# One core, two decoder layers: the first norm's row first, low-priority warm-ups, a standing VectorE, softmax sums on VectorE, twelve weight slots

## The chip, the cores and the metric

The kernel runs on one core of a Trainium2 chip. The time is device microseconds of one execution. The core's engines run their own instruction streams in order and wait for each other by semaphores: TensorE (PE; its weight loads are shown as PEld), VectorE (DVE), ScalarE (ACT), GpSimd (POOL) and SyncE (SP), which issues the DMAs.

## The reference

A decoder trunk of two layers on 256 tokens of width 1024, float32. Cut to what is computed:

```python
for layer in range(2):
    h = h + 0.5 * swiglu(rms_norm(h, ffn1_norm[layer]), ffn1_w_in[layer], ffn1_w_out[layer])
    hn = rms_norm(h, mix_norm[layer])
    if layer == 0:      # 16 heads of 64
        q, k, v = split(hn @ sb_w_qkv)
        h = h + stick_breaking_attention(q, k, v) @ sb_w_o
    else:               # 16 query heads, 4 key/value heads, window 128, one sink a head
        q = rotary(hn @ swa_w_q)
        h = h + sliding_window_sink_attention(q, k_shared, v_shared, sinks) @ swa_w_o
    h = h + 0.5 * swiglu(rms_norm(h, ffn2_norm[layer]), ffn2_w_in[layer], ffn2_w_out[layer])
    if layer == 0:
        k_shared, v_shared = rotary(k), v   # of rms_norm(h, kv_norm) @ kv_w
return rms_norm(h, final_norm)

def swiglu(x, w_in, w_out):                 # w_in 1024 x 5632, w_out 2816 x 1024
    gate, up = split(x @ w_in)
    return (silu(gate) * up) @ w_out
```

`rms_norm` is x * rsqrt(mean(x*x) + 1e-6) * gain. The softmax of the window runs over 256 keys at most, masked to the band, and the sink's logit.

## The kernel before

**Split products.** Activations and weights are split in two parts each, a high part rounded to the type fp32r and a low part that is the rest; a product is three matmuls (high x high, low x high, high x low), each 128 rows by 512 columns. A weight comes as a block of 1 MB into one of 4 `raw` slots (`RAWS`, 8 KB a partition). ScalarE copies it to the high part (`w_hi`, L324), VectorE subtracts to get the low part (`w_lo`, L326), both in two pieces of 1024 columns. The parts lie in `2 * PAIRS` = 10 slots (`WP`); a pair is released when TensorE has used it. v, q and k of the first attention, q of the second and the operands of the shared keys and values take slots of the same ten.

**Stages.** Two token tiles (t = 0, 1) of 128. A feed-forward block goes through 2816 columns in six blocks (`BLOCKS`): "p" (plain, 512), "h" (narrow, 256) and "s" (one level of Strassen over two halves of the depth and the token tiles, 512); the "s" blocks need sums of the activations' quarters, made once a layer by `make_sums` (L450 to L456). Its last two blocks' output products run tile by tile, and after each tile comes `fin`: `add_residual` (L422), `root` and `normed`.

**The norm.** `root(t)` has ScalarE square both halves with a sum (L399), VectorE add the two sums (`base`, L401) and GpSimd raise the result to the power -0.5 (`rstd`, L403). `normed` has VectorE scale each half of 512 by `rstd` and the gain (`xs`, L411); TensorE transposes it (L375), ScalarE copies the high part (L381), VectorE makes the low part (L382).

**The order.** Nothing runs in the order in which it is written. Each piece of work is a `Task` with an engine, an assumed duration, the buffers it reads and writes, and a due time `prio`. `Plan.order` plays all tasks through in time: an engine that is free takes the ready task with the smallest `prio`, never waiting for a better one, and a task becomes ready a fixed latency after those it depends on. The instruction streams are then issued in that order, and each engine keeps to it. `plan.pos` is the due time so far, which only dense matmuls advance. Splits are due 7 us ahead of it (`LEAD`), loads 30 us (`LOADS`), the Strassen sums 14 us (`SUMS`).

**The start.** Nine tasks of six warm-up matmuls each go first on TensorE (`warm_up`, due -9e5, into bank 3). SP issues the four quarters of x, the first gain row (4 KB, one partition, `grow`), the first 256 KB piece of each of the first four weight blocks, the next gain, and the other pieces. `spread` brings the row onto all 128 partitions by a matmul with a row of ones, into banks 6 and 7 (`g0`). Later gains are loaded onto all partitions by DMA (512 KB).

**The banded softmax** (`heads` in `sliding_window`): eight times for two heads, TensorE makes the scores and adds the mask, VectorE takes the maxima (L899, L900) and the negated bias (L902), ScalarE four exponentials, each with its sum (L909, `accum_out`), TensorE transposes (L918 to L920), ScalarE and VectorE copy (L386, L925), TensorE multiplies by v. After four times `outputs` adds the sink's exponential to the sums (`SM`), takes the reciprocal and scales (L948 to L955).

Of the kernel before, what the change touches and what calls it, by code (L numbers as in the profile page):

```python
# [35 lines left out]
PAIRS = 5  # L36
RAWS = 4
PIECES = 2

# [4 lines left out]
class Task:  # L44
    __slots__ = ("eng", "dur", "fn", "prio", "deps", "outs", "left", "ready", "start", "end", "seq")

    def __init__(self, eng, dur, fn, prio, seq):
# [22 lines left out]
class Plan:  # L70
# [3 lines left out]
    def add(self, eng, dur, fn, r=(), w=(), prio=None):  # L74
        t = Task(eng, dur, fn, self.pos if prio is None else prio, len(self.tasks))
        for b, k in r:
            if k in b.w:
                t.deps.add(b.w[k])
            else:
                t.deps.update(b.base)  # L80
        for b, k in w:
            if k in b.w:
                t.deps.add(b.w[k])
            else:
                t.deps.update(b.base)
# [12 lines left out]
    def order(self):
# [11 lines left out]
        while True:  # L110
# [21 lines left out]
            for o in t.outs:  # L132
                lat = 0.0 if o.eng == e and e != "SP" else LAT[e]
                o.ready = max(o.ready, t.end + lat)
                o.left -= 1
                if o.left == 0:
                    heapq.heappush(wait[o.eng], (o.ready, o.seq, o))
# [21 lines left out]
def kernel(  # L159
# [74 lines left out]
    one_row = pool.tile([1, P], F32, name="one_row")  # L234
# [6 lines left out]

    def warm_up(n):
        for i in range(n):
            mm(ps_all[:, 3, 0:S], warm.to_broadcast([P, P]), warm.to_broadcast([P, S]), True, True)
# [3 lines left out]
    for i in range(9):  # L248
        T("PE", 900, lambda: warm_up(6), r=[(consts, "warm")], w=B(banks[3]), prio=-9e5 + i)
# [39 lines left out]
    def dma(src, dst, nbytes, w, prio, name=None):  # L289
        T("SP", nbytes / 250.0, lambda: nc.sync.dma_start(out=dst(), in_=src), w=w, prio=prio)  # L290
# [103 lines left out]
    def root(t):  # L394
# [3 lines left out]
        for j in range(2):  # L398
            T("ACT", act(512), lambda j=j: ACT.activation(out=sq.ap, in_=hN.ap[:, t, half(j)], func=AF.Square, scale=1.0 / 32.0,  # L399
                                                          accum_out=ssq.ap[:, j:j + 1]), r=[(hN, (t, j))], w=[(ssq, j), (sq, 0)])  # L400
        T("DVE", 170, lambda: DVE.scalar_tensor_tensor(out=base.ap, in0=ssq.ap[:, 0:1], scalar=EPS, in1=ssq.ap[:, 1:2],  # L401
                                                       op0=ALU.add, op1=ALU.add), r=[(ssq, 0), (ssq, 1)], w=B(base))
        T("POOL", 900, lambda: POOL.tensor_tensor(out=rstd.ap, in0=base.ap, in1=mhalf, op=ALU.pow),  # L403
          r=B(base) + [(consts, "mhalf")], w=B(rstd))
# [3 lines left out]
    def normed(t, rstd, g, pair, dh, dl):  # L408
        for j in range(2):
            xs = STG.get([P, 512], F32, "xs")  # L410
            T("DVE", dve(512), lambda j=j, xs=xs: DVE.scalar_tensor_tensor(  # L411
                out=xs.ap, in0=hN.ap[:, t, half(j)], scalar=rstd.ap, in1=g.ap[:, half(j)], op0=ALU.mult, op1=ALU.mult),
                r=[(hN, (t, j))] + B(rstd, g), w=B(xs))
# [14 lines left out]
    def ffn(w_in, w_out, acc, rest, finish, kv=None, blocks=BLOCKS, first=False):  # L428
# [422 lines left out]
    def sliding_window(w_q, w_o, p0, others_, finish):  # L851
# [31 lines left out]
        def heads(g, i):  # L883
# [22 lines left out]
            for t in (1, 0):  # L906
                for par in range(2):
                    sl_ = slice(par * 384 + (1 - t) * S, par * 384 + 384 - t * P)
                    T("ACT", act(P + t * P, True) + 190, lambda t=t, par=par, sl_=sl_: ACT.activation(  # L909
                        out=e.ap[:, sl_], in_=z[par].ap[:, (1 - t) * S:384 - t * P], func=AF.Exp,  # L910
                        bias=view(NM, t, t + 1, hd + par, hd + par + 1).rearrange("p t h -> p (t h)"),
                        accum_out=view(SM, t, t + 1, hd + par, hd + par + 1).rearrange("p t h -> p (t h)")),
                        r=B(z[par]) + [nk, (consts, "tbl")], w=[(e, (par, t)), (SM, (n, par, t))])
# [26 lines left out]
        def outputs(j):  # L940
# [3 lines left out]
            SS = [(SM, (n, par, t)) for n in range(4 * j, 4 * j + 4) for par in range(2) for t in range(NT)]  # L944
# [32 lines left out]
    def load_x(t, j):  # L977
        dma(xs_[:, t, half(j)], lambda: hN.ap[:, t, half(j)], P * 512 * 4, [(hN, (t, j))], -9e5)
# [35 lines left out]
    T("POOL", 10, lambda: None, r=B(g0), w=B(banks[6], banks[7]))  # L1014
# [71 lines left out]
```

## Time and profile before

| | |
|---|---|
| median of 3 runs | 960.07 us (958.43 to 960.18) |
| profiled execution | 958.79 us, its span 957.0 us |
| mean granted TensorE clock | 0.994 |
| busy: PE, DVE, ACT, POOL | 940.1, 769.1, 566.5, 17.0 us |
| HBM read | 170.67 MB, 179 GB/s over the span |

The span runs from the first to the last instruction of the program. The busy time of an engine is the union of its instructions; matmuls are pipelined and their ends modelled, so a busy TensorE may still be slowed. "A <- B" in a list of waits says that an instruction of A was waiting until one of B had ended; the numbers behind it are the total in us, the times, and the longest. In the chain of waits, each piece is what the next one waited for, back from the end. A line number is that of the kernel before; where a helper issues many operations they share its line (L217 is every matmul).

### The profile page before, as it was taken

Reading aid. Unit: us, or ns where it says so; the run is one execution under the profiler, and the core shown is the slowest. Engines: PE = TensorE matmul, PEld = TensorE weight load, DVE = VectorE, ACT = ScalarE, POOL = GpSimd, SP = SyncE. Lnnn points to the kernel's source line nnn. Section 1 sums busy time; section 2 is a strip of 40 time slices with the busy share of each in tenths; the row PEclk is TensorE's granted clock in tenths of the full one; section 3 lists DMA queues with packets and bytes.
Section 4 is the critical chain, followed back from the end, with each engine's and each line's share of the span. In section 5 each row is a group of like instructions: output and inputs, shape, how many; then the busy total and the mean of one; then the engine's idle time right before and its main releaser. Section 6 shows DMA issues by size and latency. Waiting matters only on the chain.

```text
span 957.0 us, 11930 instructions
## 1 busy us (share of the span) xinstructions
PE 940.1 (98%) x4658; PEld 777.8 (81%) x4658; DVE 769.1 (80%) x876; ACT 566.5 (59%) x783; POOL 17.0 (2%) x30
## 2 busy tenths in 40 slices
PE   9999999999999999999999999999998999999996
PEld 6888888889897888888887888888877888888885
DVE  6888799775556998699978797899875689869993
ACT  6556467556667656556655566557745465655662
POOL 1000000000000000000000000000100000000000
PEclk8999999999999999999999999999999999999998
DMA  8929272853434537634856348256652333762441
GB/s 287 323 92 308 101 264 105 291 200 130 136 130 132 198 132 269 214 101 164 299 192 216 129 168 284 91 206 213 230 194 89 109 112 133 256 228 91 173 176 44
DMA packets 81258, 172.48 MB, mean 180 GB/s; under 512 B 3249, under 2 KB 19889, under 8 KB 81202
## 3 DMA queue, kind: packets, MB, share of 16 engines
q1 hardware_dynamic: 81202, 171.73, 52.6%
q8 instruction: 36, 0.59, 0.3%
q14 instruction: 20, 0.16, 0.0%
HBM read 170.67 MB, written 1.05 MB: 179 GB/s over the span
## 4 chain that ended last, share of the span: by engine, by line
PE 93%; DVE 4%; ACT 1%; issue 1%; POOL 0%; POOLq 0%; DVEq 0%; ACTq 0%
PE ps L217 89%; DVE w_lo L326 2%; PE ps L489 2%; PE ps L375 1%; ACT w_hi L324 0%; DVE xs L411 0%; DVE hN L422 0%; DVE xT_l L382 0%; POOL small L403 0%; DVE raw L580 0%; ACT ws L386 0%; PE ps L919 0%; PE ps L918 0%; PE ps L920 0%; DVE s L456 0%
## 5 line engine op out<-in xcount | busy, mean ns | idle before, releaser
L326 DVE TENSOR_TENSOR w_lo<-raw,w_hi 128x1024 fp32r<-128x1024 f32 x388 | 456.2, 1218 | 70.1 <-ACT w_hi L324 67.2
L324 ACT CAST w_hi<-raw 128x1024 fp32r<-128x1024 f32 x388 | 388.8, 1050 | 106.7 <-PE ps L217 52.9
L217 PE MATMUL ps<-w_hi,xT_h 128*128 128x512 f32 x528 | 210.0, 398 | 0.8 <-ACT w_hi L324 0.8
L217 PE MATMUL ps<-w_hi,xT_l 128*128 128x512 f32 x528 | 206.7, 391 | 0.9 <-DVE xT_l L382 0.9
L217 PE MATMUL ps<-w_lo,xT_h 128*128 128x512 f32 x528 | 206.7, 392 | 0.4 <-DVE w_lo L326 0.4
L217 PE MATMUL ps<-w_hi,aT_h 128*128 128x512 f32 x352 | 140.5, 399 | 0.0
L217 PE MATMUL ps<-w_lo,aT_h 128*128 128x512 f32 x352 | 137.7, 391 | 0.4 <-DVE w_lo L326 0.4
L217 PE MATMUL ps<-w_hi,aT_l 128*128 128x512 f32 x352 | 137.1, 390 | 0.0
L217 PEld LDWEIGHTS ps<-w_lo,xT_h 128*128 128x128 f32 x528 | 99.5, 188 | 22.5 <-DVE w_lo L326 1.6
L217 PEld LDWEIGHTS ps<-w_hi,xT_l 128*128 128x128 f32 x528 | 99.7, 189 | 21.5 <-DVE xT_l L382 2.0
L217 PEld LDWEIGHTS ps<-w_hi,xT_h 128*128 128x128 f32 x528 | 99.6, 189 | 21.4 <-ACT w_hi L324 1.2
L580 DVE TENSOR_TENSOR raw<-raw 128x1024 f32<-128x1024 f32 x96 | 113.8, 1216 | 0.0
L217 PEld LDWEIGHTS ps<-w_lo,aT_h 128*128 128x128 f32 x352 | 66.1, 188 | 15.1 <-DVE w_lo L326 0.9
L217 PEld LDWEIGHTS ps<-w_hi,aT_l 128*128 128x128 f32 x352 | 66.2, 188 | 12.8
L217 PEld LDWEIGHTS ps<-w_hi,aT_h 128*128 128x128 f32 x352 | 66.2, 188 | 12.5
L217 PE MATMUL ps<-w_hi,S_h 128*128 128x512 f32 x192 | 74.7, 389 | 0.0
L217 PE MATMUL ps<-w_hi,S_l 128*128 128x512 f32 x192 | 74.7, 389 | 0.0
L217 PE MATMUL ps<-w_lo,S_h 128*128 128x512 f32 x192 | 74.7, 389 | 0.0
L381 ACT CAST aT_h<-ps 128x512 fp32r<-128x512 f32 (+1 forms) x48 | 26.5, 551 | 78.5 <-PE ps L489 78.5
L477 ACT ACTIVATE m<-ps 128x512 f32<-128x512 f32 (+1 forms) x36 | 19.9, 552 | 39.0 <-PE ps L217 38.7
L217 PEld LDWEIGHTS ps<-w_lo,S_h 128*128 128x128 f32 x192 | 36.0, 188 | 7.5
L217 PEld LDWEIGHTS ps<-w_hi,S_h 128*128 128x128 f32 x192 | 36.0, 188 | 7.5
(158 smaller groups left out, 992.7 us busy)
## 6 DMA issues: line engine op xcount, KB each, us to landing
raw<-in_ffn_w_in_dram SPq DMA_DIRECT2D x76, 1024.0 KB, 5.2
raw<-in_ffn_w_out_dram SPq DMA_DIRECT2D x44, 1024.0 KB, 5.1
raw<-in_sb_w_qkv_dram SPq DMA_DIRECT2D x12, 1024.0 KB, 5.5
raw<-in_ffn_w_in_dram SPq DMA_DIRECT2D x16, 512.0 KB, 4.6
raw<-in_ffn_w_in_dram SPq DMA_DIRECT2D x16, 256.0 KB, 5.4
raw<-in_sb_w_o_dram SPq DMA_DIRECT2D x4, 1024.0 KB, 4.9
raw<-in_swa_w_q_dram SPq DMA_DIRECT2D x4, 1024.0 KB, 7.6
raw<-in_swa_w_o_dram SPq DMA_DIRECT2D x4, 1024.0 KB, 5.3
```

Of the source, the lines that this page charges most:

```text
L217: PE.matmul(ps, lhsT=lhsT, rhs=rhs, start=start, stop=stop, skip_group_check=True)
L324: T("ACT", act(m), lambda sl=sl: ACT.copy(out=flat(hi)[:, sl], in_=flat(raw)[:, sl]), r=[(raw, i) for i in ks], w=[(hi, i) for i in ks], p ...
L326: T("DVE", dve(m), lambda sl=sl: DVE.tensor_sub(out=flat(lo)[:, sl], in0=flat(raw)[:, sl], in1=flat(hi)[:, sl].bitcast(F32)), r=[(raw, i) ...
L375: PE.transpose(out=bank.ap[:, i * P:(i + 1) * P], in_=s, identity=ident)
L381: T("ACT", act(n), lambda: ACT.copy(out=hi[2](), in_=src()), r=B(bank), w=[hi[0:2]])
L477: T("ACT", act(n), lambda: ACT.activation(out=dst(), in_=src(), func=AF.Silu), r=r + [(consts, "tbl")], w=w)
L489: PE.transpose(out=tr.ap[:, i * P:(i + 1) * P], in_=m.ap[:, i * P:(i + 1) * P], identity=ident)
L580: T("DVE", dve(m), lambda sl=sl: DVE.tensor_sub(out=flat(dst)[:, sl], in0=flat(x_)[:, sl], in1=flat(y_)[:, sl]), r=[(b, k) for b in (x_, y ...
```

## The change

- **First row first.** `grow` is loaded from ScalarE's queue as that queue's first task, with a planned latency of its own (`lat`); SP's early DMAs are planned at 330 bytes per ns, and the pieces of the first weight blocks are in order of need, with x's second tile after two pieces of the first block. Gains are due 20 us after the position at which they are asked for, not 30 us before.
- **Warm-ups.** 18 tasks, 8 of two and 10 of four matmuls (56 in all, before 54), due last of all (9e5) and into bank 5; the planner places them where TensorE has nothing else ready. The 18 precede the first other use of bank 5.
- **The first feed-forward's sums** are due 5 us ahead (`FSUMS`).
- **VectorE stands still.** In `fin` the sum, the power and the scaling of the first half are one task of VectorE; its stream holds nothing between the sum and the scaling that waits for GpSimd. The norms at the very start and the final one stay as they were.
- **Banded softmax.** The exponentials have no `accum_out`; two VectorE reductions a time (512 and 256 columns), due 2 us later than their place, make the sums.
- **Twelve slots** (`PAIRS` 6). The scratch that is kept for software-made DMAs is set to 1024 bytes.
- `one_row` becomes a column of ones, broadcast; the task that frees banks 6 and 7 now also counts as a write of `g0`.

```diff
-PAIRS = 5
+PAIRS = 6
+FSUMS = 5000.0
+WARM = 18
...
-                lat = 0.0 if o.eng == e and e != "SP" else LAT[e]
+                lat = t.lat if t.lat is not None else 0.0 if o.eng == e and e != "SP" else LAT[e]
...
-            mm(ps_all[:, 3, 0:S], warm.to_broadcast([P, P]), warm.to_broadcast([P, S]), True, True)
+            mm(ps_all[:, 5, 0:S], warm.to_broadcast([P, P]), warm.to_broadcast([P, S]), True, True)
...
-    for i in range(9):
-        T("PE", 900, lambda: warm_up(6), r=[(consts, "warm")], w=B(banks[3]), prio=-9e5 + i)
+    for i in range(WARM):
+        T("PE", 430, lambda n=2 if i < 8 else 4: warm_up(n), r=[(consts, "warm")], w=B(banks[5]), prio=9e5 + i)
...
-        T("SP", nbytes / 250.0, lambda: nc.sync.dma_start(out=dst(), in_=src), w=w, prio=prio)
+        T("SP", nbytes / (330.0 if prio < -8e5 else 250.0), lambda: nc.sync.dma_start(out=dst(), in_=src), w=w, prio=prio)
...
-        dma(vec.unsqueeze(0).to_broadcast([P, D]), lambda: g.ap, P * D * 4, B(g), plan.pos - LOADS)
+        dma(vec.unsqueeze(0).to_broadcast([P, D]), lambda: g.ap, P * D * 4, B(g), plan.pos + 20000)
...
-                        [(raw, c * 2 // a)], plan.pos - LOADS if c else -8.5e5)
+                        [(raw, c * 2 // a)], plan.pos + 10 * c - 8.5e5)
...
-    def root(t):
+    def root(t, then=None):
...
-        T("DVE", 170, lambda: DVE.scalar_tensor_tensor(out=base.ap, in0=ssq.ap[:, 0:1], scalar=EPS, in1=ssq.ap[:, 1:2],
-                                                       op0=ALU.add, op1=ALU.add), r=[(ssq, 0), (ssq, 1)], w=B(base))
-        T("POOL", 900, lambda: POOL.tensor_tensor(out=rstd.ap, in0=base.ap, in1=mhalf, op=ALU.pow),
-          r=B(base) + [(consts, "mhalf")], w=B(rstd))
+        def mean():
+            DVE.scalar_tensor_tensor(out=base.ap, in0=ssq.ap[:, 0:1], scalar=EPS, in1=ssq.ap[:, 1:2], op0=ALU.add, op1=ALU.add)
+
+        def power():
+            POOL.tensor_tensor(out=rstd.ap, in0=base.ap, in1=mhalf, op=ALU.pow)
+
+        R = [(ssq, 0), (ssq, 1), (consts, "mhalf")]
+        if then:
+            dur, fn, r, w = then
+
+            def run():
+                mean()
+                power()
+                fn(rstd)
+            T("DVE", 1100 + dur, run, r=R + r, w=B(base, rstd) + w)
+        else:
+            T("DVE", 170, mean, r=R, w=B(base))
+            T("POOL", 600, power, r=B(base), w=B(rstd))
...
+            if rstd is None:
+                rstds[t] = rstd = root(t, (dve(512), scaled, [(hN, (t, j))] + B(g), B(xs)))
+            else:
+                T("DVE", dve(512), lambda scaled=scaled: scaled(rstd), r=[(hN, (t, j))] + B(rstd, g), w=B(xs))
...
-            plan.pos = at - SUMS
+            plan.pos = at - (FSUMS if first else SUMS)
...
-                    T("ACT", act(P + t * P, True) + 190, lambda t=t, par=par, sl_=sl_: ACT.activation(
+                    T("ACT", act(P + t * P, True), lambda t=t, par=par, sl_=sl_: ACT.activation(
                         out=e.ap[:, sl_], in_=z[par].ap[:, (1 - t) * S:384 - t * P], func=AF.Exp,
-                        bias=view(NM, t, t + 1, hd + par, hd + par + 1).rearrange("p t h -> p (t h)"),
-                        accum_out=view(SM, t, t + 1, hd + par, hd + par + 1).rearrange("p t h -> p (t h)")),
-                        r=B(z[par]) + [nk, (consts, "tbl")], w=[(e, (par, t)), (SM, (n, par, t))])
+                        bias=view(NM, t, t + 1, hd + par, hd + par + 1).rearrange("p t h -> p (t h)")),
+                        r=B(z[par]) + [nk, (consts, "tbl")], w=[(e, (par, t))])
+            for t in (1, 0):
+                T("DVE", dve(P * 2 + t * P * 2), lambda t=t: DVE.tensor_reduce(
+                    out=view(SM, t, t + 1, hd, hd + 2).rearrange("p t h -> p (t h)"),
+                    in_=e.ap.rearrange("p (a c) -> p a c", a=2)[:, :, (1 - t) * S:384 - t * P], axis=AX.X, op=ALU.add),
+                    r=[(e, (par, t)) for par in range(2)], w=[(SM, (n, t))], prio=plan.pos + 2000)
...
-        dma(xs_[:, t, half(j)], lambda: hN.ap[:, t, half(j)], P * 512 * 4, [(hN, (t, j))], -9e5)
+        dma(xs_[:, t, half(j)], lambda: hN.ap[:, t, half(j)], P * 512 * 4, [(hN, (t, j))], -8.5e5 + 15 if t else -9e5)
...
-    dma(ffn1_norm[0].unsqueeze(0), lambda: grow.ap, D * 4, B(grow), -8.9e5)
+    T("ACT", 60, lambda: nc.scalar.dma_start(out=grow.ap, in_=ffn1_norm[0].unsqueeze(0)), w=B(grow), prio=-9.5e5, lat=2500.0)
...
-            rstd = root(t)
-            rstds[t] = rstd
-            normed(t, rstd, g, pair, xh, xl)
+            normed(t, None, g, pair, xh, xl)
...
-    T("POOL", 10, lambda: None, r=B(g0), w=B(banks[6], banks[7]))
+    T("POOL", 10, lambda: None, w=B(g0, banks[6], banks[7]))
...
-    nc = _bacc.Bacc("TRN2", target_bir_lowering=False, num_devices=1)
+    nc = _bacc.Bacc("TRN2", target_bir_lowering=False, num_devices=1, dynamic_dma_scratch_size=1024)
```

More of the change, by code (lines that the diff above doesn't have):

```diff
@@ L35, with __init__ @@
 SUMS = 14000.0
-PAIRS = 5
+PAIRS = 6
 RAWS = 4
 PIECES = 2
+FSUMS = 5000.0
+WARM = 18
 class Task:
-    __slots__ = ("eng", "dur", "fn", "prio", "deps", "outs", "left", "ready", "start", "end", "seq")
-    def __init__(self, eng, dur, fn, prio, seq):
+    __slots__ = ("eng", "dur", "fn", "prio", "deps", "outs", "left", "ready", "start", "end", "seq", "lat")
+    def __init__(self, eng, dur, fn, prio, seq, lat):
+        self.lat = lat
         self.eng, self.dur, self.fn, self.prio, self.seq = eng, dur, fn, prio, seq
@@ L72, in __init__, with add @@
         self.tasks, self.pos = [], 0.0
-    def add(self, eng, dur, fn, r=(), w=(), prio=None):
-        t = Task(eng, dur, fn, self.pos if prio is None else prio, len(self.tasks))
+    def add(self, eng, dur, fn, r=(), w=(), prio=None, lat=None):
+        t = Task(eng, dur, fn, self.pos if prio is None else prio, len(self.tasks), lat)
         for b, k in r:
@@ L233 @@
     warm = pool.tile([P, 1], BF16, name="warm")
-    one_row = pool.tile([1, P], F32, name="one_row")
+    one = pool.tile([P, 1], F32, name="one")
     nones = pool.tile([P, P], F32R, name="nones")
@@ L410, in normed, with scaled @@
             xs = STG.get([P, 512], F32, "xs")
-            T("DVE", dve(512), lambda j=j, xs=xs: DVE.scalar_tensor_tensor(
-                out=xs.ap, in0=hN.ap[:, t, half(j)], scalar=rstd.ap, in1=g.ap[:, half(j)], op0=ALU.mult, op1=ALU.mult),
-                r=[(hN, (t, j))] + B(rstd, g), w=B(xs))
+            def scaled(rstd, j=j, xs=xs):
+                DVE.scalar_tensor_tensor(out=xs.ap, in0=hN.ap[:, t, half(j)], scalar=rstd.ap, in1=g.ap[:, half(j)], op0=ALU.mult, op1=ALU.mult)
+            if rstd is None:
+                rstds[t] = rstd = root(t, (dve(512), scaled, [(hN, (t, j))] + B(g), B(xs)))
+            else:
+                T("DVE", dve(512), lambda scaled=scaled: scaled(rstd), r=[(hN, (t, j))] + B(rstd, g), w=B(xs))
             transposes(pair[j], lambda xs=xs: [xs.ap[:, i * P:(i + 1) * P] for i in range(4)], B(xs))
@@ L943, in outputs @@
             RR = [(NM, (n,)) for n in range(4 * j, 4 * j + 4)]
-            SS = [(SM, (n, par, t)) for n in range(4 * j, 4 * j + 4) for par in range(2) for t in range(NT)]
+            SS = [(SM, (n, t)) for n in range(4 * j, 4 * j + 4) for t in range(NT)]
             def r3():
@@ L983 @@
     grow = A4.get([1, D], F32, "grow")
-    dma(ffn1_norm[0].unsqueeze(0), lambda: grow.ap, D * 4, B(grow), -8.9e5)
-    T("DVE", 100, lambda: DVE.memset(one_row, 1.0), w=[(consts, "one")], prio=-8e5)
+    T("ACT", 60, lambda: nc.scalar.dma_start(out=grow.ap, in_=ffn1_norm[0].unsqueeze(0)), w=B(grow), prio=-9.5e5, lat=2500.0)
+    T("DVE", 100, lambda: DVE.memset(one, 1.0), w=[(consts, "one")], prio=-8e5)
     g0 = Buf(lambda: ps_all[:, 6:8, :].rearrange("p a b -> p (a b)"))
@@ L989, in spread @@
         for j in range(2):
-            mm(banks[6 + j].ap, one_row, grow.ap[:, half(j)], True, True)
+            mm(banks[6 + j].ap, one[0:1].to_broadcast([1, P]), grow.ap[:, half(j)], True, True)
     T("PE", 1720, spread, r=B(grow) + [(consts, "one")], w=B(banks[6], banks[7], g0), prio=-8e5)
```

## The prediction

> **What bounds the kernel now.** The page comes first: which engine has no slack.
>
> ```profile
> PE 940.1 (98%) x4658; PEld 777.8 (81%) x4658; DVE 769.1 (80%) x876; ACT 566.5 (59%) x783; POOL 17.0 (2%) x30
> ```
>
> TensorE is busy 940.1 us, 98% of the span, and the change takes no real matmul away. So it can only win where TensorE stands still or works for nothing. The table by stretches, cut where TensorE's share falls, says where that is. Its columns after the stretch and its length are busy us of PE, PEld, DVE, ACT and POOL, the granted clock, DMA share and GB/s.
>
> ```profile
> core 0 of [0], span 957.0 us
> core 0: us, PE busy (x) PEld busy (x) DVE busy (x) ACT busy (x) POOL busy (x), PEclk, DMA share, GB/s
> 0.00:6.06 6.06, 5.13 (x25) 3.64 (x26) 1.96 (x12) 3.45 (x7) 3.47 (x17) 1.00 0.66 192
> 6.06:12.89 6.83, 6.65 (x43) 4.37 (x41) 2.28 (x5) 1.31 (x3) 0.55 (x1) 1.00 1.02 371
> 12.89:15.70 2.81, 2.06 (x9) 1.57 (x8) 2.56 (x6) 2.15 (x4) 0.00 (x0) 0.50 1.06 394
> 15.70:21.60 5.90, 5.52 (x14) 3.60 (x14) 5.90 (x8) 5.34 (x8) 0.00 (x0) 0.66 0.84 302
> 196.00:206.00 10.00, 9.14 (x42) 6.77 (x41) 8.34 (x11) 5.10 (x9) 1.40 (x1) 1.00 0.89 299
> 510.00:520.00 10.00, 8.40 (x39) 6.67 (x38) 10.00 (x12) 8.79 (x10) 0.00 (x0) 1.00 0.43 148
> 660.00:670.00 10.00, 9.57 (x42) 7.62 (x41) 10.00 (x11) 5.71 (x7) 0.00 (x0) 1.00 0.93 308
> 690.00:700.00 10.00, 8.81 (x42) 6.46 (x41) 8.87 (x14) 4.52 (x8) 2.53 (x1) 1.00 0.85 322
> 718.00:752.00 34.00, 30.91 (x225) 26.04 (x225) 19.96 (x43) 19.11 (x63) 0.00 (x0) 1.00 0.23 68
> 949.00:957.00 8.00, 0.60 (x3) 0.18 (x1) 3.28 (x6) 2.17 (x5) 0.55 (x1) 0.66 0.17 66
> ```
>
> Idle time of TensorE behind the start: 0.86 (196 to 206, into the stick-breaking layer), 1.60 (510 to 520, shared keys and values), 0.43 (660 to 670), 1.19 (690 to 700, into the sliding window), 3.09 (718 to 752, banded softmax). That is 7.2 us, the ceiling for all edits behind the start. The last 8 us are the final norm and the store, which the change leaves alone. Everything else is at the start, where "busy" misleads: warm-ups count as busy. So I follow the chain of waits there (start, length, what).
>
> ```profile
> 17.52 0.59 DVE s L456
> 18.12 0.75 DVE w_lo L326
> 19.17 0.62 DVE S_l L451
> 19.79 0.67 DVE s L456
> 20.45 1.15 DVE w_lo L326
> 21.64 17.52 PE ps L217 x76
> ```
>
> From 21.64 TensorE runs unbroken at 17.52 / 76 = 0.23 us a matmul. Before that it started 14 matmuls in 5.9 us (row 15.70 to 21.60), VectorE being busy for all 5.90; at 0.23 they need 3.2. A kernel without start trouble would have begun at 18.4, so the start costs 18.4 us, and that is the largest single item.
>
> **The start, part by part.** Lines of the timeline:
>
> ```profile
> 2.58 0.32 SPq L290 DMA_DIRECT2D grow<-in_ffn_norm_dram  x1
> ...
> 5.23 0.16 DVE L401 SCALAR_TENSOR_TENSOR small<-small 128x1 f32<-128x1 f32 x1 [1.61 <-ACT sq L399]
> ...
> 5.48 0.55 POOL L403 TENSOR_TENSOR small<-small,mhalf 128x1 f32<-128x1 f32 x1 [1.60 <-DVE small L401]
> ```
>
> and of TensorE alone:
>
> ```profile
> 0.93 8.65 PE L217 MATMUL ps<-warm 128*128 128x256 bf16 x54 [0.93 <-DVE warm L246]
> 9.50 1.98 PE L217 MATMUL ps<-grow,one_row 1*128 1x512 f32 x4
> 11.54 3.41 PE L375 MATMUL ps<-ident,xs 128*128 128x128 f32 x16
> 15.72 0.80 PE L217 MATMUL ps<-w_hi,xT_h 128*128 128x512 f32 x1 [0.77 <-ACT w_hi L324]
> ```
>
> The first power is there at 5.48 + 0.55 = 6.03, but the gain row, which TensorE spreads over all partitions, waits in TensorE's queue behind 54 warm-ups until 9.50. The change gives warm-ups the lowest priority, so the order puts the spread as soon as the row is due: with the planner's own costs (row at 2560, warm-up 430, spread 1720 ns), after six warm-up tasks. They hold 12 matmuls. At 5.13 / 25 = 0.21 us each from 0.93 they end at 3.5.
>
> When the row lands no line shows. It is now the first thing in ScalarE's queue, ahead of the table load, instead of SP's fifth (2.58). The nearest row is a quarter of x:
>
> ```profile
> hN<-in_x_dram SPq DMA_DIRECT2D x4, 256.0 KB, 3.3
> ```
>
> 4 KB should not take longer than these 256 KB, so 0.7 + 3.3 = 4.0 at the latest; 3.5 is the earliest that counts. The spread takes 1.98 at full clock and up to 4.0 at half, and ends between 5.5 and 7.5.
>
> Walking on through the planner's costs I get 32 warm-up matmuls and 8 transposes between the spread and the first real matmul, and 12 more warm-ups and 8 transposes within the first real ones. A warm-up takes 0.21 at the early pace and (9.50 - 6.06) / 29 = 0.12 after 6.06. Transposes are 3.41 / 16 = 0.21. Full clock: 5.5 + 32 x 0.12 + 1.7 = 11.0; then 14 matmuls 3.2, transposes 1.7, warm-ups 1.4 make 17.3 against 21.64: a gain of 4.3. Half clock all the way: 7.5 + 32 x 0.21 + 1.7 = 15.9, no earlier than now; staying at half until 19.72 as now, the 6.3 us of full-clock work would end near 24.1: a loss of 2.5. Between them: now the faster pace came 5.1 us after the warm-ups began (0.93 to 6.06); begun again at 7.5 it comes at 12.6, the first matmul at 14.3, and 20.6 is the end: a gain of 1.0.
>
> VectorE supports the early side. The first Strassen sums drop from 14 to 5 us of lead, so 0.59 + 0.62 + 0.67 = 1.9 us leave its chain ahead of the weight parts; the order of the first weight pieces by need, with x's second half behind two of them, and the 512 KB of the next gain moved away from their front, help the same way. The queue it moves past is SP's own:
>
> ```profile
> SPq L290 <- DVE w_lo L326: 761.3, 146, 22.5
> ```
>
> SP waits 761.3 us for raw slots; the gains now go into those gaps, each long before its norm, so nothing is late by it. I take 3.0, nearer to the upper end because of those 1.9 us.
>
> The smaller DMA scratch pays for the two new slots; the page's queues show hardware-made DMAs and instruction fetches alone, so I cost it at nothing.
>
> **The standing still.** One norm seam, 691.98 on, VectorE and GpSimd:
>
> ```profile
> 691.98 0.15 DVE L401 SCALAR_TENSOR_TENSOR small<-small 128x1 f32<-128x1 f32 x1
> 692.05 2.35 DVE L326 TENSOR_TENSOR w_lo<-raw,w_hi 128x1024 fp32r<-128x1024 f32 x2
> 692.28 2.53 POOL L403 TENSOR_TENSOR small<-small,mhalf 128x1 f32<-128x1 f32 x1 [7.46 <-DVE small L401]
> 694.85 1.41 DVE L411 SCALAR_TENSOR_TENSOR xs<-hN,small,gain 128x512 f32<-128x512 f32 x2 [0.44 <-POOL small L403]
> ```
>
> The power takes 0.55 beside an idle VectorE (at 5.48) and 2.53 beside two weight parts. From mean to first scaled half is 2.87 us; standing still it is 6.03 - 5.23 = 0.8 plus a hop, 0.9. The half comes up to 2.0 us sooner, more than the 1.19 and 0.86 that TensorE idles at the two t=1 seams. The price: 0.7 us of VectorE, ten times. Queued behind it are low weight parts, and who waits for those is TensorE; the cover is VectorE's slack (8.34 and 8.87 of 10 in these stretches). Also, weight parts due earlier than the norm still go first, so not all 2.0 us arrive. Ends: 0 and 2.05 for both; I take 1.5 with the slots below.
>
> [...]
>
> **Twelve slots.** One more hi/lo pair lets one more 1 MB weight be split ahead.
>
> ```profile
> ACT w_hi L324 <- PE ps L217: 52.9, 42, 2.8
> ```
>
> ```profile
> PE ps L489 <- DVE m L480: 1.6, 1, 1.6
> ```
>
> ScalarE's splits wait 52.9 us, 42 times, for TensorE, which is when slots come free. A pair is two parts of 2.35 us (row 692.05) moved ahead. At 510 to 520 VectorE is busy 10.00 of 10 and its late product m stops TensorE for 1.6; 2.35 us less in front would remove it, two stand-stills 10 and 20 us earlier put 1.4 back. Ends: 0 and 2.03 with the 0.43 at 660; I take 1.3.
>
> **Banded softmax.** From the groups:
>
> ```profile
> L909 ACT ACTIVATION_READ_ACCUMULATOR e<-ps,small 128x1 f32 x32 | 6.7, 210 | 0.0
> L899 DVE TENSOR_REDUCE small<-ps 128x2 f32<-128x512 f32 x8 | 5.5, 691 | 8.4 <-PE ps L217 8.3
> L900 DVE TENSOR_REDUCE small<-ps 128x2 f32<-128x256 f32 x8 | 3.3, 414 | 0.0
> ```
>
> ScalarE loses 32 reads, 6.7 us at most; VectorE gains 8 x (0.69 + 0.41) = 8.8, by the same-sized maxima. Both have room (19.96 and 19.11 of 34), so it is latency: the exponentials of a pair end up to 0.8 sooner, while a sum can hold up the next maximum by 0.69, and each half's last sums (1.1) lie before the reciprocal. Ends: a gain of 3.09 (the whole hole) and a loss of 3.0 (a sum of 0.4 before each of eight maxima, less what idles). I take a gain of 0.5.
>
> **Sum.** 3.0 + 1.5 + 1.3 + 0.5 = 6.3. The profiled execution took 958.79 in all, span 957.0 and 1.8 around it; 958.79 - 6.3 = 952.5. The median of the runs is 1.3 above the profiled one, so 953.8.
>
> **Rivals.**
> Late clock: the warm-ups run at half pace and delay what they should help. The spread has one row of weights, and after it and the transposes the clock was at 0.50 (12.89 to 15.70), which speaks for it; that the warm-ups are many speaks against. The start gives 1.0 or less, the rest 2.3: 960.1 - 3.3 = 956.8. [...]
>
> The seams do not move: four raw slots, not weight slots, limit the lead, and stand-still and slots cancel. For it: VectorE is full exactly where TensorE waits at 510. Against it: the 42 waits. Only the start's 3.0 is left: 957.1. With a late clock besides, no change: 959.5.
>
> VectorE becomes the bound, slower. It gets 8.8 us of sums and 7 of stand-still, 16 us more. Place: the stretches with 10.00 of 10 busy and the softmax. From the point where the pair's 2.35 us of lead is used up, each stand-still is TensorE's wait: ten of 0.7, and half of the sums, 4.4, with the start giving 3: 960.1 + 7.0 + 4.4 - 3.0 = 968.5. Against: 188 us of VectorE idle.
>
> **How the numbers follow.** A measurement of this kernel tells 0.2%, 1.9 us, from no change. Forecast 0.58, late clock 0.16, unmoved seams 0.12, neither (959.5) 0.07, slower 0.07. Faster: forecast, and most of the next two: 0.82. Same: 0.11. Slower: 0.07. Range: low end with start 4.3 and all but the softmax's last 2 us of the 7.2: 960.1 - 9.5 = 950.6, less 1.6 for matmuls that are only slow, 949.0; high end between the unmoved seams and no change, 959.0.
>
> **What would show it.** Right: the gain row's spread before 5, the first real matmul before 13, TensorE unbroken from about 18.5; powers all at 0.55; the wait for m at 510 to 520 under 0.6; no accumulator reads in the softmax and its idle time under 3. Wrong: a granted clock of 0.50 past 13, TensorE waiting for low weight parts just behind a norm, or more idle than 3.1 us in the softmax.

## The result, and the profile after

The changed kernel takes 950.62 us (median of 4 executions, 947.73 to 951.12) against 959.29 us for the kernel before on the same chip (4 executions, 958.43 to 960.18). The ratio is 0.9903, 95% interval 0.988 to 0.9927. The forecast was 953.8 in a range of 949.0 to 959.0. The profiled execution is the fastest of the four: 947.73 us, span 945.9, against 958.79 before, a gain of 11.06. The medians differ by 8.67.

The page first (busy us, share of the span, instructions).

```profile
PE 934.0 (99%) x4660; PEld 775.8 (82%) x4660; DVE 775.4 (82%) x892; ACT 561.4 (59%) x751; POOL 10.6 (1%) x30
```

VectorE does 6.3 us more than before, ScalarE 5.1 and GpSimd 6.4 less. The table by stretches of the changed kernel, cut at the same pieces of work (columns as before: stretch, length, busy us of PE, PEld, DVE, ACT and POOL, granted clock, DMA share, GB/s):

```profile
core 0 of [0], span 945.9 us
...
4.04:12.75 8.71, 8.05 (x61) 5.99 (x60) 4.57 (x9) 5.06 (x12) 1.10 (x2) 1.00 0.95 328
12.75:18.00 5.25, 5.25 (x26) 4.37 (x24) 5.21 (x7) 4.70 (x7) 0.00 (x0) 1.00 1.05 391
190.00:200.00 10.00, 9.47 (x45) 7.46 (x44) 9.27 (x13) 5.82 (x10) 0.55 (x1) 1.00 0.55 180
510.00:520.00 10.00, 9.12 (x47) 7.30 (x46) 8.21 (x10) 4.86 (x7) 0.00 (x0) 1.00 0.90 320
655.00:665.00 10.00, 10.00 (x47) 8.30 (x47) 9.42 (x10) 5.00 (x6) 0.00 (x0) 1.00 1.02 378
682.00:692.00 10.00, 9.53 (x46) 7.54 (x45) 8.61 (x15) 6.37 (x11) 0.55 (x1) 1.00 0.73 236
710.00:744.00 34.00, 33.28 (x241) 28.17 (x238) 27.46 (x57) 17.18 (x39) 0.00 (x0) 1.00 0.20 62
```

Against before, TensorE's idle time fell from 0.86 to 0.53 at the stick-breaking seam, from 1.60 to 0.88 at m, from 0.43 to nothing, from 1.19 to 0.47 at the sliding window's seam, and from 3.09 to 0.72 in the banded softmax. From the first real matmul at 12.75 TensorE is busy without a break (5.25 of 5.25).

To split the gain without judging by eye I use one marker: number 100, counted from 0, of the matmuls that read a high weight part.

```profile
core 0 of [0], span 945.9 us
...
48.56 0.39 PE L220 MATMUL ps<-w_hi,aT_h 128*128 128x512 f32 x1
```

That is TensorE's timeline after; before, the same matmul stands at 53.81. What comes before it I call the start. From its start to the start of the last such matmul I call the body: 889.35 after, 895.17 before. The rest, 8.03 to 8.05 us, is the same in every run. So the gain is 53.81 - 48.56 = 5.25 of start and 5.82 of body, 11.07 in all.

The start in the changed kernel, from its timeline (start, length, engine, what):

```profile
0.73 0.52 ACTq L1012 DMA_DIRECT2D grow<-in_ffn_norm_dram  x1
...
0.92 2.75 PE L220 MATMUL ps<-warm 128*128 128x256 bf16 x12 [0.92 <-DVE one L1013]
...
3.60 2.18 PE L220 MATMUL ps<-grow,one 1*128 1x512 f32 x4
...
5.71 1.96 PE L220 MATMUL ps<-warm 128*128 128x256 bf16 x16
...
8.81 0.63 ACT L404 ACTIVATE sq<-hN 128x512 bf16<-128x512 f32 x1 [0.56 <-DMA hN<-in_x_dram]
8.83 1.95 PE L220 MATMUL ps<-warm 128*128 128x256 bf16 x16
...
9.44 0.57 ACT L385 CAST xT_h<-ps 128x512 fp32r<-128x512 f32 x1
...
11.94 1.06 PE L220 MATMUL ps<-warm 128*128 128x256 bf16 x8
...
12.75 0.47 PE L220 MATMUL ps<-w_hi,xT_h 128*128 128x512 f32 x1
```

The spread starts at 3.60 instead of 9.50. After it come 16 warm-ups in 1.96 us, 0.12 each, which is the fast pace. All 44 warm-ups behind the spread (16, 4, 16 and 8) stand ahead of the first real matmul. ScalarE's first split of x^T waits behind the squares of x's second tile (8.81 before 9.44). In SP's queue that tile follows one piece of the first weight block (issued at 1.65, the tile at 2.71), not two, as the change was meant to have it: the planner put the block's second piece behind the landing that it assumed for the first (e8 undoes this).

### The profile page after: what moved, and what is told of

Its sections match the earlier page's. It is cut to its first block, busy times and chain, and to the rows that moved or that the text cites. A ratio compares the mean times of both kernels' runs of the same rounds, so it can differ in the third digit from the quotient of the medians.

```text
span 945.9 us, 11893 instructions
## 1 busy us (share of the span) xinstructions
PE 934.0 (99%) x4660; PEld 775.8 (82%) x4660; DVE 775.4 (82%) x892; ACT 561.4 (59%) x751; POOL 10.6 (1%) x30
## 4 chain that ended last, share of the span: by engine, by line
PE 96%; DVE 2%; DMA 1%; ACT 0%; issue 0%; SPq 0%; POOLq 0%; POOL 0%; DVEq 0%; ACTq 0%
PE ps L220 92%; PE ps L513 2%; PE ps L379 1%; DVE w_lo L330 1%; DMA hN<-in_x_dram 1%; DVE xT_l L386 0%; DVE hN L446 0%; DVE xs L433 0%; SPq L294 0%; PE ps L946 0%; PE ps L948 0%; PE ps L947 0%; ACT xT_h L385 0%; ACT sq L404 0%; ACT hg L1068 0%
## 5 line engine op out<-in xcount | busy, mean ns | idle before, releaser
L386 DVE TENSOR_TENSOR aT_l<-ps,aT_h 128x512 fp32r<-128x512 f32 (+1 forms) x48 | 30.8, 642 | 14.0 <-ACT aT_h L385 13.9
```

The costliest lines, as they stand in the source:

```text
L386: T("DVE", dve(n), lambda: DVE.tensor_sub(out=lo[2](), in0=src(), in1=hi[2]().bitcast(F32)), r=B(bank) + [hi[0:2]], w=[lo[0:2]])
```

## The experiments

Every kernel below computes the whole result; warm-ups are no part of it. Full clock is the moment of the first record of a full granted clock in the profiled execution; first, start and body are that execution's too. Each ratio is to executions of the kernel before on the same chip; their medians are 959.29 for the changed kernel and 958.41 to 958.57 for e1 to e12, so the ratios compare better than the medians.

| kernel | median us (lowest to highest, executions) | ratio to before, 95% | full clock | first real matmul | start | body |
|---|---|---|---|---|---|---|
| before | 959.29 (958.43-960.18, 4) | | 6.06 | 15.72 | 53.81 | 895.17 |
| changed | 950.62 (947.73-951.12, 4) | 0.9903, 0.988-0.9927 | 4.04 | 12.75 | 48.56 | 889.35 |
| e1 start alone | 954.64 (951.04-955.34, 6) | 0.9952, 0.9938-0.9966 | 10.12 | 14.78 | 50.60 | 893.58 |
| e2 ten slots | 952.52 (949.28-953.18, 6) | 0.9931, 0.9918-0.9943 | 11.57 | 15.48 | 51.28 | 891.42 |
| e3 no standing still | 956.28 (952.32-959.05, 9) | 0.9973, 0.9956-0.9989 | 12.73 | 16.05 | 51.87 | 894.60 |
| e4 sums on ScalarE | 950.40 (948.87-952.48, 6) | 0.9915, 0.9901-0.9929 | 4.27 | 12.64 | 48.45 | 891.07 |
| e5 old start | 952.81 (952.0-953.07, 5) | 0.9937, 0.9923-0.995 | 6.78 | 15.82 | 53.94 | 889.30 |
| e6 no warm-ups | 948.25 (947.49-948.3, 4) | 0.989, 0.9876-0.9903 | 15.44 | 11.55 | 49.13 | 889.35 |
| e7 warm-ups first | 950.91 (950.69-951.22, 4) | 0.9919, 0.9906-0.9933 | 6.83 | 13.65 | 50.97 | 890.44 |
| e8 true landings | 950.81 (950.02-951.85, 4) | 0.9919, 0.9905-0.9932 | 12.91 | 15.70 | 51.96 | 890.08 |
| e9 e6 and e8 | 950.38 (949.56-950.71, 4) | 0.9913, 0.9897-0.9928 | 14.65 | 9.22 | 50.30 | 890.13 |
| e10 e8, warm-ups priced truly | 950.89 (949.84-951.99, 4) | 0.9919, 0.9906-0.9933 | 11.85 | 12.06 | 51.08 | 890.18 |
| e11 ten slots, no standing still | 952.15 (949.79-953.15, 5) | 0.993, 0.9917-0.9942 | 4.37 | 12.35 | 48.14 | 891.81 |
| e12 e6, row on SP | 947.95 (947.71-949.0, 4) | 0.9891, 0.9877-0.9904 | 16.76 | 11.72 | 49.88 | 889.27 |

Medians mix two things: the body, which the order of the work sets, and the moment at which the clock is granted, with which the first real matmul moves by up to 3.7 us among the profiled executions with the changed kernel's order of warm-ups (12.35 to 16.05). Two executions of e3 (958.77 and 959.05) lost about 2.5 us more than its profiled one, at a mean clock of 0.995 instead of 0.998. So the parts are told apart by the bodies. Each body is that of one execution. That it doesn't hang on the clock's moment, e5, e6 and e12 show: their clock rose otherwise (at 6.78 and, after falling back at 13.61, again at 20.44; at 15.44; at 16.76), and their bodies are the changed kernel's to 0.08. In the kernel before, too, the clock fell back, from 12.89 to 19.72.

### One part at a time: e1 to e5, e11

e1 keeps the start's edits alone. Ten slots, no standing still, sums on ScalarE:

```diff
-PAIRS = 6
+PAIRS = 5
...
-            normed(t, None, g, pair, xh, xl)
+            rstds[t] = root(t)
+            normed(t, rstds[t], g, pair, xh, xl)
...
-                    T("ACT", act(P + t * P, True), lambda t=t, par=par, sl_=sl_: ACT.activation(
+                    T("ACT", act(P + t * P, True) + 190, lambda t=t, par=par, sl_=sl_: ACT.activation(
...
+                        accum_out=view(SM, t, t + 1, hd + par, hd + par + 1).rearrange("p t h -> p (t h)")),
```

> The changed kernel with ten slots, the exponentials' sums back on ScalarE and the old root/normed in the norm seams: only the start (row, warm-ups, order of the first loads, sums' lead, later gains) is left of the change. Theory A (the start gives over half): 3 to 6 us under the kernel before, ratio 0.994 to 0.997, and TensorE's idle time behind the start near the 7.2 us of before. Rival (the start is worth little in the median because of a late clock, the other parts carry the gain): 0 to 1.5 us under the kernel before, ratio 0.9985 to 1.000.

e1's ratio, 0.9952, is 4.6 us under the kernel before, inside theory A's range; 1.59 us of it lie in the body. e2 undoes the slots alone (the first two lines of that diff), e3 the standing still alone (the next three), e4 the sums alone (the rest, with the two reductions gone).

> The changed kernel with ten slots instead of twelve. Theory A: the waits of 510 to 520 and 660 to 670 come back, 1.1 us above the changed kernel, and with ten slots the norm seams lose some too, 1 to 2 us in all (ratio to the kernel before about 0.992). Rival (raw slots limit the lead): no difference to the changed kernel, 0.9903.

> The changed kernel with the norm's sum, power and scaling as separate tasks again. Theory A: the power beside weight parts takes 1.4 to 2.5 us again, TensorE's idle time at the two t=1 seams goes from 1.0 to about 2 us: 1 us slower than the changed kernel. Rival (twelve slots alone closed the seams): no difference, or up to 1 us faster, since VectorE does not stand for 7 us.

> The changed kernel with the exponentials' sums back on ScalarE. Theory A: the softmax's idle time of TensorE goes from 0.7 back towards 3.1 us, 2.4 us slower than the changed kernel. Rival (the slots or the order made the softmax shorter): less than 0.7 us of difference, softmax idle near 0.7.

TensorE's waits in e1 (waiting line, what it waited for, us in total, times, longest):

```profile
PE ps L220 <- ACT ws L390: 1.5, 2, 1.0
PE ps L220 <- ACT qT L390: 1.1, 1, 1.1
...
PE ps L513 <- DVE m L504: 0.8, 1, 0.8
```

The same view of the changed kernel:

```profile
PE ps L513 <- DVE m L504: 0.9, 1, 0.9
...
PE ps L220 <- ACT ws L390: 0.6, 1, 0.6
```

The wait for m was 1.6 before and is 0.8 in e1, which has none of the slots: there neither slots nor standing still took it down. But neither are the start's edits needed: e5, with the old start under the other parts, has a wait of 0.9 for m. What is left in e1 lies in the softmax (ws, the transposed weights, and qT), 2.6 of it, and 2.0 of that is gone in the changed kernel.

e4 against the changed kernel isolates the sums: 891.07 - 889.35 = 1.72 us. The softmax of e4, from its table by stretches:

```profile
712.00:746.00 34.00, 31.88 (x226) 26.83 (x225) 20.32 (x44) 18.61 (x62) 0.00 (x0) 1.00 0.26 85
```

TensorE's longest wait in e4, from its waits:

```profile
PE ps L220 <- ACT ws L390: 1.4, 1, 1.4
```

TensorE idles 2.12 there against 0.72, and its longest wait is for ScalarE's copy of the transposed weights, on the engine that has the accumulator reads back. e4's median is still that of the changed kernel: by their times, half of its executions had an early clock (948.87, 949.21, 949.34; the last is the profiled one), and one of four of the changed kernel's.

e3 was the surprise: without the standing still, the body is 5.25 longer than the changed kernel's. In its waits the norm's scaled half stands first:

```profile
PE ps L379 <- DVE xs L433: 2.7, 2, 1.4
PE ps L513 <- DVE m L504: 1.5, 1, 1.5
```

The seam into the stick-breaking layer, from e3's timeline:

```profile
196.45 2.50 DVE L330 TENSOR_TENSOR w_lo<-raw,w_hi 128x1024 fp32r<-128x1024 f32 x2
...
198.13 0.19 ACT L404 ACTIVATION_READ_ACCUMULATOR sq<-hN 128x1 f32 x1
...
198.87 0.15 DVE L408 SCALAR_TENSOR_TENSOR small<-small 128x1 f32<-128x1 f32 x1
...
199.17 0.55 POOL L411 TENSOR_TENSOR small<-small,mhalf 128x1 f32<-128x1 f32 x1 [10.51 <-DVE small L408]
...
199.29 1.23 DVE L330 TENSOR_TENSOR w_lo<-raw,w_hi 128x1024 fp32r<-128x1024 f32 x1 [0.27 <-ACT w_hi L328]
...
200.43 0.75 DVE L433 SCALAR_TENSOR_TENSOR xs<-hN,small,gain 128x512 f32<-128x512 f32 x1
```

The same seam in the changed kernel's timeline:

```profile
192.98 0.19 ACT L404 ACTIVATION_READ_ACCUMULATOR sq<-hN 128x1 f32 x1
...
193.24 0.15 DVE L408 SCALAR_TENSOR_TENSOR small<-small 128x1 f32<-128x1 f32 x1
...
193.54 0.55 POOL L411 TENSOR_TENSOR small<-small,mhalf 128x1 f32<-128x1 f32 x1 [8.19 <-DVE small L408]
...
194.12 1.42 DVE L433 SCALAR_TENSOR_TENSOR xs<-hN,small,gain 128x512 f32<-128x512 f32 x2 [0.73 <-POOL small L411]
```

In e3 the power takes 0.55 as well, with a weight part that starts 0.12 after it. The half is late all the same, because weight parts stand on VectorE ahead of the mean (to 198.9) and between power and scaling (199.29). From the end of the last square's read to the scaling it takes 198.32 to 200.43, 2.1 us; in the changed kernel 0.95. My theory then was that with twelve slots more weight parts are ready just then, and that the planner, which takes what is ready, puts them in that gap. e11 asks whether ten slots without standing still have the same loss:

```diff
-PAIRS = 6
+PAIRS = 5
...
-            normed(t, None, g, pair, xh, xl)
+            rstds[t] = root(t)
+            normed(t, rstds[t], g, pair, xh, xl)
```

> The changed kernel with ten slots and without the standing still (start and softmax sums stay). Theory E (more slots put more ready weight parts in front of the norm's scaling, so that twelve slots pay only with the standing still): TensorE's time from the 100th weight matmul to the last is 893 to 894 us, less than the 894.6 with twelve slots and no standing. Rival (slots pay by themselves, 2 us): 896 or more.

It measures 891.81: no such loss, 2.79 less than e3, and still less than the theory had given. At the same seam, e11's timeline:

```profile
194.19 0.16 DVE L408 SCALAR_TENSOR_TENSOR small<-small 128x1 f32<-128x1 f32 x1
194.26 1.22 DVE L330 TENSOR_TENSOR w_lo<-raw,w_hi 128x1024 fp32r<-128x1024 f32 x1
194.50 1.40 POOL L411 TENSOR_TENSOR small<-small,mhalf 128x1 f32<-128x1 f32 x1 [9.74 <-DVE small L408]
195.93 1.42 DVE L433 SCALAR_TENSOR_TENSOR xs<-hN,small,gain 128x512 f32<-128x512 f32 x2 [0.44 <-POOL small L411]
```

Here one weight part runs beside the power, which takes 1.40, and mean to scaling is 1.74 against 0.88 standing still. From the end of the last square's read it is 2.05, hardly less than e3's 2.1. So this tile doesn't show what the slots cost. The first token tile, just before, does. VectorE in e3:

```profile
186.67 1.22 DVE L330 TENSOR_TENSOR w_lo<-raw,w_hi 128x1024 fp32r<-128x1024 f32 x1
187.81 0.15 DVE L408 SCALAR_TENSOR_TENSOR small<-small 128x1 f32<-128x1 f32 x1
188.97 1.23 DVE L330 TENSOR_TENSOR w_lo<-raw,w_hi 128x1024 fp32r<-128x1024 f32 x1 [1.01 <-ACT w_hi L328]
190.11 1.41 DVE L433 SCALAR_TENSOR_TENSOR xs<-hN,small,gain 128x512 f32<-128x512 f32 x2
```

and in e11:

```profile
183.90 0.16 DVE L408 SCALAR_TENSOR_TENSOR small<-small 128x1 f32<-128x1 f32 x1 [0.87 <-ACT sq L404]
184.79 1.42 DVE L433 SCALAR_TENSOR_TENSOR xs<-hN,small,gain 128x512 f32<-128x512 f32 x2 [0.73 <-POOL small L411]
```

With ten slots VectorE stands idle before the mean and before the scaling, as nothing else is ready. With twelve a weight part fills each gap, and the scaling comes 2.5 us after the last read instead of 0.9. Over the ten norms that the standing still touches, the way from read to scaling adds up, counted from the timelines, to 16.7 us in e11, with 12 weight parts on VectorE meanwhile, and to 20.7 in e3, with 16; standing still it is 10.2 with ten slots and 10.9 with twelve. TensorE's waits account for the loss: for the scaled half 2.7 in e3 against 0.6 in e11, for m 1.5 against 0.8, together 2.8. The bodies so give a table of two by two:

| body, us | ten slots | twelve slots |
|---|---|---|
| VectorE goes on | 891.81 (e11) | 894.60 (e3) |
| VectorE stands still | 891.42 (e2) | 889.35 (changed) |

Standing still is worth 0.39 with ten slots and 5.25 with twelve. Two more slots lose 2.79 without it and win 2.07 with it. Together they give 2.46. The fastest executions of the four, 949.79 (e11), 952.32 (e3), 949.28 (e2) and 947.73 (changed), say the same in smaller measure: standing still is worth 0.51 with ten slots and 4.59 with twelve, and two more slots lose 2.53 without it and win 1.55 with it.

e5 puts the old start back under the three other parts (warm-ups first and 54, the row on SP, the old order and due times of early loads and gains):

```diff
-    for i in range(WARM):
-        T("PE", 430, lambda n=2 if i < 8 else 4: warm_up(n), r=[(consts, "warm")], w=B(banks[5]), prio=9e5 + i)
+    for i in range(9):
+        T("PE", 900, lambda: warm_up(6), r=[(consts, "warm")], w=B(banks[3]), prio=-9e5 + i)
...
-            plan.pos = at - (FSUMS if first else SUMS)
+            plan.pos = at - SUMS
...
-    T("ACT", 60, lambda: nc.scalar.dma_start(out=grow.ap, in_=ffn1_norm[0].unsqueeze(0)), w=B(grow), prio=-9.5e5, lat=2500.0)
+    dma(ffn1_norm[0].unsqueeze(0), lambda: grow.ap, D * 4, B(grow), -8.9e5)
```

> The changed kernel with the old start (54 warm-ups first, the row fifth in SP's queue, old order of loads, old lead of the sums and gains). Theory A (start and body add up): first real matmul at 15.7, TensorE's holes behind the start as in the changed kernel (about 4), so 3.9 us slower than the changed kernel, about 954 where the kernel before is 958.5. Rival (the planner reshuffles the body so that parts do not add): the body's holes are nearer to the 11 of before, 956 or more.

Its ratio is 0.0034 above the changed kernel's, 3.3 us, and its body (889.30) is the changed kernel's to 0.05. So start and body add up. The start's edits alone (e1) also took 1.59 us from the body, but with the other parts there that is nothing more: it is the same idle time. The smaller scratch and the small rewrites (`one`, banks 6 and 7) stay in e1 to e12, so no run tells their worth apart.

### The warm-ups and the clock: e6, e7, e12

With twelve warm-ups ahead of the spread the full clock came at 4.04, 4.27 and 4.37 in three profiled executions (changed, e4, e11) and at 10.12, 11.57, 11.85, 12.73 and 12.91 in five others (e1, e2, e10, e3, e8), with one order of TensorE's work up to the spread. The first real matmul came at 12.35 to 12.75 or at 14.78 to 16.05 accordingly (at 12.06 in e10, which has only 16 warm-ups behind the spread). TensorE's timeline in e3, a late one:

```profile
3.60 3.78 PE L220 MATMUL ps<-grow,one 1*128 1x512 f32 x4
7.31 3.59 PE L220 MATMUL ps<-warm 128*128 128x256 bf16 x16
...
16.05 0.47 PE L220 MATMUL ps<-w_hi,xT_h 128*128 128x512 f32 x1
```

Spread and warm-ups run at half pace (16 in 3.59 us, not 1.96), and the real work queues behind them. "Phase" in the expectations from here on is whether the clock came early, as at 4.04, or late, as here at 12.73. e6 leaves the warm-ups out:

```diff
-WARM = 18
+WARM = 0
```

> The changed kernel with no warm-up at all. [...] Rival (the warm-ups are free in any phase): at least 3 us slower than the changed kernel's median, 953.5 or more where the kernel before is 958.5.

TensorE's timeline in e6:

```profile
2.21 3.75 PE L220 MATMUL ps<-grow,one 1*128 1x512 f32 x4 [2.21 <-DVE ntri L276]
6.95 1.97 PE L379 MATMUL ps<-ident,xs 128*128 128x128 f32 x8 [0.99 <-DVE xs L433]
10.79 1.12 PE L379 MATMUL ps<-ident,xs 128*128 128x128 f32 x4 [1.86 <-DVE xs L433]
11.55 0.78 PE L220 MATMUL ps<-w_hi,xT_h 128*128 128x512 f32 x1
```

Everything here runs at half pace (the spread takes 3.75 us, against 1.98 in e7), the first record of the full clock is at 15.44, and the first real matmul is still 1.2 earlier than in the changed kernel's early case. The body is the same (889.35), the start 49.13 is 0.57 later than that early case and 1.5 to 2.7 earlier than the late ones of e1 to e3. Its four executions lie within 0.8 us, and all are below the changed kernel's other three. So the rival, at least 3 us above the changed kernel's median, is refuted, and that it would be faster than the changed kernel's late executions was not expected. e7 puts 28 warm-ups ahead of the spread and 28 behind it as fillers:

```diff
-    for i in range(WARM):
-        T("PE", 430, lambda n=2 if i < 8 else 4: warm_up(n), r=[(consts, "warm")], w=B(banks[5]), prio=9e5 + i)
+    for i in range(14):
+        T("PE", 430, lambda: warm_up(2), r=[(consts, "warm")], w=B(banks[5]), prio=-9e5 + i)
+    for i in range(7):
+        T("PE", 430, lambda: warm_up(4), r=[(consts, "warm")], w=B(banks[5]), prio=9e5 + i)
```

> The changed kernel with 28 warm-up matmuls unbroken from the start (0.9 to about 6.5), then the row's spread, then 28 as fill. [...] Rival (the scatter comes from the loads, not the clock): scatter stays, and the later spread makes it 1 to 2 us slower.

The clock came at 6.83 and the scatter fell to 0.5 us, which the rival had stay, but the spread starts at 6.95, the first real matmul at 13.65, TensorE waits 0.74 for VectorE's low part of x^T up to 18.06, and the body is 1.1 longer, with waits of 0.29 and 1.02 near 200. The median, 950.91, is that of the changed kernel (950.62); the ratio is 0.0016 above, 1.5 us, inside the rival's loss, but the intervals overlap. e12 asks whether the row's own queue matters, without warm-ups:

```diff
-WARM = 18
+WARM = 0
...
-    T("ACT", 60, lambda: nc.scalar.dma_start(out=grow.ap, in_=ffn1_norm[0].unsqueeze(0)), w=B(grow), prio=-9.5e5, lat=2500.0)
+    dma(ffn1_norm[0].unsqueeze(0), lambda: grow.ap, D * 4, B(grow), -8.9e5)
```

> No warm-ups, and the gain row from SP's queue behind x's first tile instead of from ScalarE's queue. If the row's queue matters, the spread starts 1.5 to 3 us later than the 2.2 without warm-ups, the first scaled half waits for it, and the time is 1 to 2 us above the run without warm-ups (ratio 0.990 to 0.991). Rival (the row only has to be there by 6, when the power is): no difference, 0.989.

It does not: the spread starts at 4.10 instead of 2.21, and the median, 947.95, is that of e6 within 0.3. Without warm-ups, then, the row's queue doesn't matter; the row on SP's queue with the warm-ups as fillers was not run, so that the row needed only a way past the warm-ups is inferred.

### A truer plan of the start: e8, e9, e10

The planner has the early loads land otherwise than the trace does; e8 gives it latencies nearer to the measured ones, e9 does so without warm-ups, e10 with 28 warm-ups in pairs, and the spread at 3.6 us (at half pace it took 3.75 in e6).

```diff
-        T("SP", nbytes / (330.0 if prio < -8e5 else 250.0), lambda: nc.sync.dma_start(out=dst(), in_=src), w=w, prio=prio)
+        T("SP", nbytes / (390.0 if prio < -8e5 else 250.0), lambda: nc.sync.dma_start(out=dst(), in_=src), w=w, prio=prio,
+          lat=2900.0 if prio < -8.9e5 else 4650.0 if prio < -8e5 else None)
...
-                        [(raw, c * 2 // a)], plan.pos + 10 * c - 8.5e5)
+                        [(raw, (c * 2 // a, c % 2) if c % 2 else c * 2 // a)], plan.pos + 10 * c - 8.5e5)
```

> The changed kernel with the landings of the first loads planned as the trace shows them (4.65 us after the issue instead of 2.0, the second piece of a block no longer planned behind the landing of the first). Theory D (ScalarE's squares of the second tile, which wait for x until 8.8, stand in front of the first high part at 9.44 and delay the first real matmul): the high part moves to about 8.2 and the first real matmul is 0.5 to 1.2 us earlier at the same clock phase. Rival (the warm-ups in front decide): no earlier than 12.6 in an early phase, same time as the changed kernel.

> No warm-ups, and the first loads' landings planned as the trace shows them. [...]

> 28 warm-up matmuls in tasks of two (0.43 us at half clock, as planned), the spread planned at 3.6 us as at half clock, landings as measured: warm-ups that fill holes without lengthening them. [...] Rival (warm-ups help in no phase once loads and VectorE pace the start): equal to or slower than no warm-ups, 0.989 or more.

None is better. e8's first real matmul comes 0.35 us earlier than e3's at the like moment of the clock (15.70 and 16.05), though the high part, expected at 8.2, came at 12.64. In e9 it comes earliest of all, at 9.22, but then waits, from its timeline:

```profile
9.22 0.79 PE L220 MATMUL ps<-w_hi,xT_h 128*128 128x512 f32 x1 [0.56 <-ACT xT_h L386]
10.59 0.79 PE L220 MATMUL ps<-w_hi,xT_l 128*128 128x512 f32 x1 [0.58 <-DVE xT_l L387]
```

and VectorE's product m comes late: TensorE waits for it for 1.55 up to 36.12, and for 2.51 up to 36.88 in e10. The bodies of e8 to e10 are 0.7 to 0.8 longer as well, with a wait of 1.02 or 1.03 for VectorE's low part of x^T near 200; why the plan moves there stays open. Starting earlier than VectorE's work can follow gained nothing.

## Why the prediction was right, and where it was wrong

**The start (3.0).** Right in the median, 3.3 by e5, but in part by luck: it is a mean over two cases, early and late clock, and the prediction took one number near the early case's. The profiled execution gained 5.25 where the early end gave 4.3; the late ones of e1 to e3 gained 1.9 to 3.2 where the late case gave 1.0. The spread came at 3.60, as worked out (3.5), and the row was there by 2.21 in e6, so the bound of 4.0 by a 256 KB load was loose. The order of the warm-ups was counted wrong: 44 and not 32 stand between spread and first real matmul, and none within the first real ones. So that matmul came at 12.75, not 11.0, but TensorE did not break off after it, and that more than paid.

**The late clock, a rival at 0.16, is what happened in most executions.** Its mechanism was right (16 warm-ups behind the spread take 3.59 us in e3 and 1.96 in the changed kernel), and the price between the two cases, 4.3 - 1.0 = 3.3, met the measured one, with a slip in it: until 12.6 only 24 of the 32 warm-ups fit at 0.21, the other eight at 0.12 add 1.0, and the first matmul would come at 15.3 instead of 14.3, with no gain at the start and a price of 4.3. Three of the changed kernel's four executions took 2.7 to 3.4 us more than the profiled one, and the late starts of e1 to e3 are 2.0 to 3.3 later than 48.56. That the changed kernel's three were late ones is inferred from their times, as only one execution has a trace. Its time of 956.8 was not reached because the body gave 5.8, not 2.3; by the prediction's own terms the rest is 1.5 + 1.3 + 0.5 = 3.3, which makes that time 955.8. The records of the granted clock before change at 6.06, 12.89 and 19.72, and in e5 at 6.78, 13.61 and 20.44: 6.83 apart in both. With one order of work up to the spread, and 12 warm-ups lasting 2.75 us ahead of it, the grant came early in three of eight profiled executions (4.04 to 4.37) and late in five (10.12 to 12.91). What decides between the two no run shows.

**Standing still (1.5) and twelve slots (1.3).** Their sum, 2.8, stands against 2.46 measured. As two terms that add up they were wrong: alone they give 0.39 and -2.79. The step that failed is "One more hi/lo pair lets one more 1 MB weight be split ahead" with 0 as its low end: a loss was left out, though the prediction itself noted that weight parts go ahead of the norm. The places were half right: of the waits that it named, the 0.43 at 660 went with the slots (0.4 in e2, none in the changed kernel), the one for m did not (0.8 in e2, 0.9); most of the slots' 2.07 came in the softmax, where e2 waits 0.7 for qT and 0.6 for VectorE's copy of ws and the changed kernel does not. The size of the standing still was taken from the worst seam, 2.87 from mean to scaling; at the seam in e11 it was 1.74, and 0.88 after. The powers all took 0.55 in the changed kernel, as expected. A power took 1.40 beside one weight part in e11, 2.53 beside two in the kernel before, and 0.55 in e3, where the weight part started 0.12 after it; why a weight part can lengthen it no run shows.

**m.** Wrong. The wait was to fall under 0.6 through the pair's lead of 2.35 us; it is 0.9, and e1 shows 0.8 without the slots. Why the start's edits move it in e1, the gains' later loads or another order of the plan, and why the other parts do the same without them in e5, stays open.

**The banded softmax (0.5).** The mechanism was right, the term too small: 1.72 (e4) and 1.77 (893.58 - 891.81, e1 to e11). The loss that was set against it, sums holding up the maxima, does not show in TensorE's idle time; VectorE is busy for 27.46 of the 34 us. The rest of the fall from 3.09 to 0.72 came with slots and standing still together: 2.12 is left in e4, against 3.09 before with the same softmax.

**The total.** The profiled gain was 11.06 instead of 6.3: 2.25 more at the start (an early clock), 1.2 more in the softmax, and 1.6 of body that the start's edits bring alone, less 0.3 from seams and slots. This split holds for one order of adding the parts: start, softmax sums, then slots and standing still (1.59 + 1.77 + 2.46 = 5.82). Added last, the start's edits take nothing from the body (e5). That VectorE becomes the bound, the slower rival, is refuted for the changed kernel (775.4 us, 82%); in e3, with the slots and without the standing still, VectorE's order does cost TensorE time, by weight parts in front of a norm.

## What to carry to other kernels

Two edits that use the same slack have to be measured two by two: more buffers let a greedy order put ready bulk work in front of short, urgent work, and here they paid only once that gap was closed. Warm-up matmuls cost their place in the queue (first real matmul at 12.06 to 16.05 with them, at 9.22 to 11.72 without), and here, where the start waits for loads, they came too late to be repaid in most executions; leaving them out gave 948.25 and 947.95 us, against 950.62, and less scatter (the intervals of their ratios overlap with the changed kernel's, so this gain over it is likely rather than shown). Where executions scatter, compare stretches of the trace behind the disturbed one, not totals.

## What the runs showed that was not expected

The moment of the grant: one order of work got its full clock at 4.0 to 4.4 or at 10.1 to 12.9 us, and its first real matmul moved by up to 3.7 us with it. A single row of 4 KB, issued at 0.73 on ScalarE's queue, had landed by 2.21 in e6, within 1.5 us. And half clock at the start was cheap here: e6 runs at half pace until 15.44 and is only 0.57 us behind the changed kernel's early start, and 0.99 behind the best of all (48.14, e11).
